# Rows of gathered experts placed by an estimate of VectorE's spare time, through the mixer and the dense experts

## The chip, the cores and the metric

The kernel runs on one core of a Trainium2 chip. A core has TensorE (PE, with its weight loads as PEld), VectorE (DVE), ScalarE (ACT), GpSimd (POOL) and SyncE (SP), each with an instruction queue of its own that is worked off in order, and 16 DMA engines that all of them share. The metric is the device time of one execution in microseconds (us), as the median of the runs.

## The reference

One layer of a decoder with 1024 tokens of 1024 channels, then a final norm:

```
h = rms_norm(x)
x = x + hybrid_mixer(h)          # stick-breaking attention, sparse attention, HGRN2, merge gates, w_out
h = rms_norm(x)
x = x + peer_ffn(h)
out = rms_norm(x)

# peer_ffn: 16384 experts, each a row of u_tab and a row of v_tab; 8 heads pick 16 experts each for every token
eidx, gate = ...                               # 128 experts a token, by the product of two key lists
hpre = einsum("nd,nhkd->nhk", xc, u_tab[eidx])
act  = gate * gelu(hpre)
y    = einsum("nhk,nhkd->nd", act, v_tab[eidx])
```

## The kernel before

**Parts.** The tokens are four parts of 256 (`PARTS`), that is eight tiles of 128. The parts go through the mixer one after the other, interleaved in 492 steps. In each step a few stages of the attention chains are emitted, and then further pieces (projections, norms, key scores, routes) up to a budget of VectorE and TensorE work.

**Two ways through the experts.** The middle parts (`DENSE`, tiles 2 to 5) go through all 16384 experts on TensorE. There are 128 first keys, and each takes one `gemm1` (24 matmuls of 512 columns, L242), splits of the weights into two float16 halves on ScalarE and VectorE (L200, L201), a product with the spread gates (L1368), and 24 matmuls of `gemm2` (L1375). Every fourth key adds a part kept in SBUF (L1383). At the end come four small final norms (L1395, L1398). The outer parts (tiles 0, 1, 6 and 7) gather their experts instead: for each of a tile's 128 choices one indirect DMA on GpSimd's queue brings 128 rows of 1024 floats (512 KB), one row for each token, and one VectorE instruction uses them. Such a transfer with its instruction is called a row here. A tile has 128 rows of `u` (L1104 and L1106) and then 128 of `v` (L1114 and L1116), so the four tiles have 1024 rows, all of which are emitted last in the program:

```
for c in range(128):
    vr = rows(f"v{ti}_{c}")                                   # one of RB = 5 buffers
    G.indirect_dma_start(out=vr, ..., in_=a["peer_v"], ...)   # L1114
    with paced():
        V.scalar_tensor_tensor(acc, in0=vr, scalar=act[:, c:c + 1], in1=acc, ...)   # L1116
```

The accumulator `acc` (called gacc in the profile) and, during the `u` rows, the tile's activations (gh) come from the same five buffers, so four are left for rows in flight. After a tile's last `v` row come its final norm and one store (L1119, L1120).

**What sets the order.** Each engine's order is fixed when the program is built: a scheduler with estimated times places the instructions, and emission order is their priority, so the rows come last in rank. `paced()` gives each row's VectorE instruction a lower bound: it may not stand ahead of a given VectorE instruction, the last one of some step. `mark()` is called at the end of each step and records that instruction with the step's estimated VectorE work `v` and TensorE work `p`. In the kernel before, `paced()` spreads 420 rows (`PACE`) over the mixer's steps from 135 on in proportion to `p + 3.0`, and leaves the other 604 with the mixer's last step as their only bound.

Tiles 0 and 1 know their experts after the first part's routes, which run beside the second part's mixer. Tiles 6 and 7 know theirs only when the last part's remaining pieces (merge, output projection, key scores, routes) have run, which is among the first keys of the dense experts.

Of the kernel before, what the change touches and what calls it, by code (L numbers as in the profile page):

```python
# [10 lines left out]
F32 = mybir.dt.float32  # L11
F16 = mybir.dt.float16
# [9 lines left out]
# the tensor and vector engines' work (us) that a step of the mixer is filled up to; the tensor engine's after the  # L22
# last step, and as a multiple of the vector engine's
RPE, RDVE, REND, PD = 3.5, 3.0, 5.0, 1.2
# the gathered rows that go beside the mixer: from which step on, how many, and a step's share besides its products
PACE0, PACE, PB = 135, 420, 3.0
# steps of the last part's tail for each block of dense experts; how far the first products run ahead
TP, LEAD = 3, 3
# buffers: gathered rows, weights, small tiles; banks for logits and transposes
# [7 lines left out]
# operands of the large products are split into two float16 parts after scaling by these powers of two  # L37
# [4 lines left out]
# scales of the gates, of their spread over the experts, and of the activations in the dense experts  # L42
# [5 lines left out]
# block numbers in the stream of projection weights  # L48
# [5 lines left out]
class Part:  # L54
    """a run of tokens that goes through the mixer together"""
# [8 lines left out]
# the parts whose tokens go through all experts; the others' experts are gathered  # L64
# [5 lines left out]
def trunk(ctx: ExitStack, tc: tile.TileContext, a: dict, out: bass.AP):  # L70
# [13 lines left out]
    # what the mixer alone needs  # L84
# [8 lines left out]
    def log_exp():  # L93
        """the activation table that holds both the logarithm and the exponential"""
        tc.keep_in_program_order(S.preload_act_table_set(LOG_EXP))
# [11 lines left out]
    def PT(shape, name):  # L107
        """a bank for transposes"""
        if mixing[0]:
            return ps_tr.tile(list(shape), F32, tag="tr", name=name)  # L110
        return ps_mm.tile(list(shape), F32, tag="mm", name=name)
# [17 lines left out]
    # strictly causal block in reversed key order: key 127 - x, allowed where 127 - x < p  # L129
# [3 lines left out]
    # causal block: key x allowed where p - x >= 0  # L133
# [3 lines left out]
    # for each length of segments: keys of a first half before queries of the second, the second halves' queries only  # L137
# [7 lines left out]
    # distances to the keys of the window and to the ends of the blocks, negative; far under where the key isn't seen  # L145
# [11 lines left out]
    # lower bounds: cumulative softmax over the layers less the first layer's share  # L157
# [12 lines left out]
    # the window's keys and values: this part's and the one's before  # L170
# [27 lines left out]
    def split(hi, lo, src, scale):  # L198
        """src * scale in two float16 parts"""
        S.activation(hi, src, AF.Copy, scale=scale)  # L200
        V.scalar_tensor_tensor(lo, in0=src, scalar=scale, in1=hi, op0=ALU.mult, op1=ALU.subtract)  # L201

    def rms_scale(src, name, junk, tg=""):
        """1/sqrt(mean(src^2) + eps) for each of 128 rows of 1024."""
# [15 lines left out]
    def load_w(blk, name, pt, br=False):  # L220
        """a block of weights in two parts; split for the first part, kept in DRAM for the others"""
# [29 lines left out]
    def transposed(src, name, pre=False):  # L251
        """the 128-column blocks of src transposed, side by side in one bank"""
# [11 lines left out]
    def norm_rows(xt, gname, nm):  # L264
        """RMSNorm of one token tile"""
        ht = W4(f"ht_{nm}")
        y = rms_scale(xt, nm, ht)
        V.scalar_tensor_tensor(ht, in0=xt, scalar=y, in1=gbc[gname], op0=ALU.mult, op1=ALU.mult)
        return ht

    def norm_cols(ht, hh, hl, tl, kk, scale, nm):
        """half of a token tile transposed into columns of hh / hl"""
# [24 lines left out]
    # Work comes in two kinds. Pieces stand on their own (projections, norms, merges); items are steps of the  # L297
    # branches' chains, each cut into four stages so that several can be under way at once.
# [37 lines left out]
    def sb_pieces(p, pt, st):  # L336
# [3 lines left out]
        def keep(t, d):  # L340
            # the tokens of earlier parts come back from DRAM
# [10 lines left out]
        # keys and values in reversed token order  # L352
# [19 lines left out]
    def sb_items(p, pt, st):  # L372
# [3 lines left out]
        def chunk(tl, hh, c0, c1, W):  # L376
# [17 lines left out]
            def weights():  # L394
                ee = x["ee"]
                # sum of softplus from the last key down, the key itself included
# [42 lines left out]
    def nsa_kv_pieces(pt, st):  # L439
# [22 lines left out]
        # compression of keys and values: block c takes the pieces c and c + 1 of 16 tokens.  # L462
        # Two neighbouring positions lie one under the other on the partitions; columns: position pair, group, block
# [3 lines left out]
        def pieces(which):  # L467
# [13 lines left out]
            # the last piece is kept for the next part  # L481
# [35 lines left out]
    def nsa_q_pieces(g, pt, st):  # L517
        gn = f"ns{pt.i}g{g}"

        def pq(i):  # L520
            # over the head's slope, a power of two: the distances then come in whole numbers, the same for all heads
# [8 lines left out]
    def nsa_items(g, tl, pt, st, kv):  # L530
# [9 lines left out]
        # compressed branch  # L540
        def c_logits():
# [6 lines left out]
            # a column of nothing before the first block  # L548
# [19 lines left out]
        def c_select():  # L568
            # importance of the blocks: the heads' weights of the five pieces that overlap; sure blocks at the top
# [7 lines left out]
            # the four best are struck out, by value and place  # L577
# [6 lines left out]
        def c_rows():  # L584
            # the block bias and the distance penalty as further rows of the queries
# [18 lines left out]
        # the selection is found and used while the window's heads go on  # L604
        res = [[c_logits, c_norm, c_turn, c_values], [None, c_select, None, None], None, [None, None, c_rows, None]]

        # window branch, then selected branch, one head at a time
        sums = {}

        def head(br, i):  # L610
# [9 lines left out]
            def logits():  # L620
# [3 lines left out]
                # logits, negative, and the least of them  # L624
# [77 lines left out]
    def hg_pieces(h, pt, st):  # L702
        """projections of a head: values token-major; gates raw"""
# [21 lines left out]
    def hg_items(h, pt, st):  # L725
# [10 lines left out]
        def decays():  # L736
            f = k = st["raw"][:, 0]
            V.tensor_scalar(f, f, olower[:, h:h + 1], lower[:, h:h + 1], op0=ALU.mult, op1=ALU.add)
            # log f; where f lies under the range of the logarithm's table, of f scaled up
# [25 lines left out]
        # attention within a chunk, by halves of ever shorter segments  # L765
        def level(lv):
# [7 lines left out]
            def spans():  # L774
                # both sides' distances to the middle
# [6 lines left out]
            def products():  # L782
                # keys on the first halves, queries (which lie n further) on the second
# [21 lines left out]
        # decays to the chunk's end and from its start  # L805
# [27 lines left out]
        # norm over the channels of the head, output gate  # L833
# [18 lines left out]
    def gate_pieces(r, pt, st):  # L852
        """six of the merge gates, raw"""
# [9 lines left out]
    def sigmoids(hg, mg, ng):  # L863
        """the sigmoids of a head of HGRN2, of six merge gates and of the sparse attention's gates, under one table"""
# [19 lines left out]
    def tail_pieces(pt):  # L884
# [17 lines left out]
        def wo(j):  # L902
            if j == 0:
                # at the end a buffer of the norm's is free
# [32 lines left out]
    def score_pieces(pt, st):  # L937
# [8 lines left out]
        def pq2(h):  # L946
# [3 lines left out]
            # the sixteen best of 128 and their places, in order  # L950
# [19 lines left out]
    def route(tile_no, ts_, ti_, gate):  # L970
        """best keys [128, 8, 2, 16] and their numbers -> first and second key of every expert [128, 128], gates [128, 8, 16]"""
# [9 lines left out]
        for h0 in (0, 4):  # L981
            # sums of the pairs (a, b) that can be among the sixteen best: all with (a + 1) * (b + 1) <= 16
# [18 lines left out]
        # gates  # L1001
# [7 lines left out]
        # place in the list -> (a, b)  # L1009
        V.tensor_copy(pf, p2)  # L1010
        # 0..31: a = pos >> 4, b = pos & 15
# [4 lines left out]
        # from 32: a = (pos >> 3) - 2, b = pos & 7; from 48: a = (pos >> 2) - 8, b = pos & 3; from 64: a = pos - 56, b = 0  # L1016
# [9 lines left out]
        # keys' numbers at (a, b): one-hot products, all whole numbers under 128  # L1026
# [27 lines left out]
    def account():  # L1054
        """estimates of what the vector and tensor engines have been given since the last call (us)"""
# [8 lines left out]
    total_ = [0.0, 0.0]  # L1064

    def mark():
        """a step's work: the vector engine's last instruction, and what the vector and tensor engines have to do"""
        account()
        v, p = load_["DVE"] - total_[0], load_["PE"] - total_[1]
        total_[:] = load_["DVE"], load_["PE"]  # L1070
        marks.append((next(i for i in reversed(nc.cur_bb.bb.instructions) if i.engine == mybir.EngineType.DVE), v, p))
# [3 lines left out]
    def paced():  # L1075
        """the next row's arithmetic waits for its turn among the mixer's"""
        if not paces:
            def rows(tau):
                return [tau * (p + PB) if k >= PACE0 else 0.0 for k, (_, v, p) in enumerate(marks)]

            lo, hi = 0.0, 10.0
            for _ in range(40):
                mid = (lo + hi) / 2
                lo, hi = (mid, hi) if sum(rows(mid)) < PACE else (lo, mid)
            acc = 0.0
            for m, r in zip(marks, rows(lo)):
                acc += r
# [408 lines left out]
```

## Time and profile before

| | |
|---|---|
| median of 3 runs | 3744.84 us |
| lowest and highest run | 3733.98 and 3757.71 us |
| profiled execution, first to last instruction | 3722.6 us |
| granted TensorE clock, mean | 0.921 |
| busy: TensorE, VectorE, ScalarE, GpSimd | 3285.9, 3035.8, 1572.2, 1275.4 us |
| moved by DMA | 1055.48 MB, 284 GB/s on average |

The profile is of one execution. Its span counts from the first to the last instruction; its own device time is not among the numbers at hand, and the three runs lie 11 to 35 us over the span. Engines overlap, so the busy times don't add up: what matters is which of them is full, or waited for, in each stretch. The mixer fills the time up to about 2100 us, then comes a stretch in which the last part's tail and the first dense keys mix, and from about 2490 us to 3676 us dense experts and gathered rows run side by side.

### The profile page before, as it was taken

The numbers are of one execution on the slowest core, as the hardware profiler recorded it, in microseconds if no ns is written. First come the engines' busy times: TensorE is split into PE (matmuls) and PEld (weight loads), VectorE is DVE, ScalarE is ACT, GpSimd is POOL, SyncE is SP. The second block draws the span as 40 slices with busy tenths as digits, with TensorE's granted clock in tenths as the row PEclk, the third lists the DMA queues.
The fourth block names the chain that finished last, engine by engine and source line by source line (L and its number), as shares of the span: only waits on it lengthen the run. The fifth ranks groups of instructions, "written<-read, shape, count | busy, mean of one in ns | idle before, by whom it ended". The sixth has DMA issues, their size and how long they took to land. (4 is left out here: it accounts for less than half of the span.)

```text
span 3722.6 us, 57637 instructions
## 1 busy us (share of the span) xinstructions
PE 3285.9 (88%) x20660; PEld 2191.0 (59%) x20660; DVE 3035.8 (82%) x7067; ACT 1572.2 (42%) x3110; POOL 1275.4 (34%) x1167
## 2 busy tenths in 40 slices
PE   6999999999986999898878897859999999999993
PEld 5887777777875777786566453424444444444441
DVE  5665689788799888789988678988888887888886
ACT  4776456554444564554457223323232223223222
POOL 0000002343322432233222344144555554555554
PEclk9999999999995999898577999979999999999996
DMA  7964857889974878877465999579999999999987
GB/s 260 334 243 144 295 189 274 317 308 325 328 273 147 300 256 300 296 278 261 142 208 195 356 332 325 193 273 339 333 337 325 320 337 322 346 332 318 334 287 261
DMA packets 359916, 1055.48 MB, mean 284 GB/s; under 512 B 35814, under 2 KB 108330, under 8 KB 355532
## 3 DMA queue, kind: packets, MB, share of 16 engines
q0 software_dynamic: 147456, 536.94, 41.5%
q1 hardware_dynamic: 212172, 514.86, 38.7%
q8 instruction: 162, 2.65, 0.3%
q14 instruction: 126, 1.03, 0.1%
HBM read 943.66 MB, written 108.00 MB: 283 GB/s over the span
## 5 line engine op out<-in xcount | busy, mean ns | idle before, releaser
L1114 POOL DMA_INDIRECT v<-in_peer_v_dram,gidx x512 | 655.1, 1280 | 872.7 <-DVE gacc L1116 590.8
L1104 POOL DMA_INDIRECT u<-in_peer_u_dram,gidx x512 | 605.9, 1183 | 869.1 <-DVE u L1106 599.4
L242 PE MATMUL g<-h,us 128*128 128x512 f16 x3072 | 712.5, 390 | 109.0 <-DVE acc L1383 71.4
L1116 DVE SCALAR_TENSOR_TENSOR gacc<-v,act,gacc 128x1024 f32<-128x1024 f32 x512 | 654.6, 1278 | 112.2 <-DMA v<-in_peer_v_dram,gidx 104.8
L1106 DVE SCALAR_TENSOR_TENSOR u<-u,gh 128x1024 f32<-128x1024 f32 x512 | 618.1, 1219 | 124.6 <-DMA u<-in_peer_u_dram,gidx 123.2
L242 PEld LDWEIGHTS <-us 128*128 128x128 f16 x3072 | 306.1, 100 | 497.8 <-issue 115.4
L1375 PE MATMUL acc<-vs,ac 128*128 128x512 f16 x2304 | 536.3, 384 | 33.1 <-ACT ac L200 28.4
L1375 PEld LDWEIGHTS <-ac 128*128 128x128 f16 x3072 | 302.9, 99 | 414.2 <-ACT ac L200 30.9
L242 PE MATMUL pj_mg<-hT,w_mg 128*128 128x256 f16 x2304 | 279.1, 277 | 16.3 <-ACT mg L859 9.5
L242 PEld LDWEIGHTS <-w_mg 128*128 128x128 f16 x2304 | 229.5, 101 | 48.8 <-issue 20.7
L200 ACT ACTIVATE vs<-vraw 128x1024 f16<-128x1024 f32 x128 | 133.8, 1048 | 270.3 <-DMA vraw<-in_peer_v_dram 270.1
L200 ACT ACTIVATE ac<-ge 128x512 f16<-128x512 f32 x128 | 79.9, 626 | 365.8 <-DVE ge L1368 250.0
L1335 ACT ACTIVATE ge<-g 128x512 f32<-128x512 f32 x128 | 75.6, 590 | 362.7 <-PE g L242 362.6
L1375 PE MATMUL g<-vs,ac 128*128 128x512 f16 x768 | 179.5, 385 | 9.6 <-DVE ts L958 7.3
L201 DVE SCALAR_TENSOR_TENSOR vs<-vraw,vs 128x1024 f16<-128x1024 f32 x128 | 155.2, 1217 | 23.2 <-ACT vs L200 23.2
L1174 PE MATMUL gb<-hot 128*128 128x128 f16 x512 | 126.3, 295 | 44.6 <-ACT stage L1177 28.9
L1177 ACT ACTIVATE stage<-gb 128x512 f32<-128x512 f32 x128 | 131.9, 1070 | 79.0 <-DMA d_G<-stage 45.2
L200 ACT ACTIVATE us<-uraw 128x1024 f16<-128x1024 f32 x128 | 134.0, 1049 | 68.2 <-DMA uraw<-in_peer_uT_dram 52.6
L242 PE MATMUL pb<-o,w_b 128*128 128x256 f16 x1152 | 141.6, 279 | 19.4 <-DMA w_b<-dw 9.3
L201 DVE SCALAR_TENSOR_TENSOR us<-uraw,us 128x1024 f16<-128x1024 f32 x128 | 155.7, 1218 | 2.9 <-ACT us L200 2.7
L242 PE MATMUL pj_r_hg<-hT,w_r_hg 128*128 128x256 f16 x1152 | 138.2, 277 | 1.5 <-ACT iv_hg L715 0.7
L242 PEld LDWEIGHTS <-w_b 128*128 128x128 f16 x1152 | 113.8, 101 | 42.6 <-issue 14.5
(1133 smaller groups left out, 5944.0 us busy)
## 6 DMA issues: line engine op xcount, KB each, us to landing
uraw<-in_peer_uT_dram SPq DMA_DIRECT2D x128, 512.0 KB, 6.7
vraw<-in_peer_v_dram SPq DMA_DIRECT2D x128, 512.0 KB, 6.2
w_mg<-dw SPq DMA_DIRECT2D x72, 512.0 KB, 6.3
d_G<-stage SPq DMA_DIRECT2D x32, 1024.0 KB, 5.1
gt<-d_G SPq DMA_DIRECT2D x32, 1024.0 KB, 13.2
w_r_hg<-dw SPq DMA_DIRECT2D x36, 512.0 KB, 5.7
w_b<-dw SPq DMA_DIRECT2D x72, 256.0 KB, 5.9
wr_mg<-in_wblk_dram SPq DMA_DIRECT2D x24, 512.0 KB, 5.1
```

The source lines that it names most:

```text
L200: S.activation(hi, src, AF.Copy, scale=scale)
L201: V.scalar_tensor_tensor(lo, in0=src, scalar=scale, in1=hi, op0=ALU.mult, op1=ALU.subtract)
L242: P.matmul(ps, l[:, k, :], r[:, k, :], start=(i == 0), stop=(i == n - 1))
L1104: G.indirect_dma_start(out=ur, out_offset=None, in_=a["peer_u"], in_offset=bass.IndirectOffsetOnAxis(ap=idx[:, c:c + 1], axis=0))
L1106: V.scalar_tensor_tensor(ur, in0=ur, scalar=1.0, in1=h2, op0=ALU.mult, op1=ALU.mult, accum_out=hpre[:, c:c + 1])
L1114: G.indirect_dma_start(out=vr, out_offset=None, in_=a["peer_v"], in_offset=bass.IndirectOffsetOnAxis(ap=idx[:, c:c + 1], axis=0))
L1116: V.scalar_tensor_tensor(acc, in0=vr, scalar=act[:, c:c + 1], in1=acc, op0=ALU.mult, op1=ALU.add)
L1174: P.matmul(ps[:, n, :], hs[:, 0, :, n], hs[:, 2, :, n], start=True, stop=False)
L1177: S.activation(stage[0][:, :, m0:m0 + 4].rearrange("p i n -> p n i"), ps, AF.Copy, scale=SA / SGT)
L1335: S.activation(ge, ps, AF.Gelu, scale=1.0 / (SW * SH2))
L1375: P.matmul(ps, ac[:, x, t * 128:(t + 1) * 128], v[:, y, dh * 512:(dh + 1) * 512], start=start and n == 0, stop=stop and n == 2)
```

## The change

`mark()` gets estimates of its own for each instruction, `paced()` a new rule, and marks are also set in the dense part: one ahead of it, and three for each first key (after `gemm1`, after the splits and the gate product, after `gemm2`). The new rule takes for each step the surplus of TensorE's estimated work over VectorE's, `max(p - v, 0)`, over the first 97% of all steps (`ROWS_BY`), multiplies it with one factor for all steps, and lets rows come in that proportion, never more than those whose experts are known by then (256 for each tile that has been routed). The factor is the smallest that brings all 1024 rows in. Rows beyond the list are bound to the step at 97%. No instruction is added, removed or changed; what can change is where the rows, and what the scheduler places around them, stand in each engine's order.

The core of the diff (comments that were taken out, and the constants `PACE0`, `PACE`, `PB` that fall away, are left out):

```diff
+ROWS_BY = 0.97
 def mark():
-    account()
-    v, p = load_["DVE"] - total_[0], load_["PE"] - total_[1]
-    total_[:] = load_["DVE"], load_["PE"]
-    marks.append((next(i for i in reversed(nc.cur_bb.bb.instructions) if i.engine == mybir.EngineType.DVE), v, p))
+    ins = nc.cur_bb.bb.instructions
+    v = p = 0.0
+    for i in ins[marked[0]:]:
+        if i.engine == mybir.EngineType.DVE:
+            aps = [x for x in [*i.outs, *i.ins] if len(getattr(x, "ap", ())) > 1]
+            n = max([math.prod([x[1] for x in o.ap[1:]]) for o in aps] or [0])
+            v += 0.09 + n / (1920.0 if aps and all(o.dtype in (F16, BF16) for o in aps) else 960.0)
+        elif i.engine == mybir.EngineType.PE:
+            n = math.prod([x[1] for x in i.outs[0].ap[1:]])
+            if i.ins[0].dtype != F32:
+                p += max(n / 2340.0, 0.11)
+            else:
+                p += 0.11 if getattr(i, "is_transpose", False) else 2 * max(n / 1170.0, 0.105)
+    marked[0] = len(ins)
+    marks.append((next(i for i in reversed(ins) if i.engine == mybir.EngineType.DVE), v, p))
 def paced():
     if not paces:
-        def rows(tau):
-            return [tau * (p + PB) if k >= PACE0 else 0.0 for k, (_, v, p) in enumerate(marks)]
-        lo, hi = 0.0, 10.0
+        spare = [max(p - v, 0.0) for _, v, p in marks[:int(len(marks) * ROWS_BY)]]
+        known = [256 * sum(r < k for r in known_.values()) for k in range(len(spare))]
+        def fill(f):
+            acc, res = 0.0, []
+            for w, n in zip(spare, known):
+                acc = min(acc + f * w, n)
+                res.append(acc)
+            return res
+        lo, hi = 0.0, 4.0
         for _ in range(40):
             mid = (lo + hi) / 2
-            lo, hi = (mid, hi) if sum(rows(mid)) < PACE else (lo, mid)
-        acc = 0.0
-        for m, r in zip(marks, rows(lo)):
-            acc += r
-            paces.extend([m[0]] * (int(acc) - len(paces)))
-        paces.append(marks[-1][0])
+            lo, hi = (mid, hi) if fill(mid)[-1] < 256 * len(known_) - 0.5 else (lo, mid)
+        for m, r in zip(marks, fill(hi)):
+            paces.extend([m[0]] * (int(r) - len(paces)))
+        paces.append(marks[len(spare)][0])
         paces.append(0)
...
     if pt not in DENSE:                       # routes(): a gathered tile's experts are known
         nc.sync.dma_start(d_gate[ti], gate)
+        known_[ti] = len(marks) + 2
...
+mark()                                        # ahead of the dense experts
 for k, i in enumerate(order):
     if k + LEAD < NI:
         ges[order[k + LEAD]] = gemm1(order[k + LEAD])
+        mark()
...
     split(ac[:, 0], ac[:, 1], ge, 1.0)
     group.append((ac, v))
+    mark()
...
     gone += 1
+    mark()                                    # after gemm2
```

More of the change, by code (lines that the diff above doesn't have):

```diff
@@ L24 @@
 RPE, RDVE, REND, PD = 3.5, 3.0, 5.0, 1.2
-PACE0, PACE, PB = 135, 420, 3.0
+ROWS_BY = 0.97
 TP, LEAD = 3, 3
@@ L1062, in account @@
         seen[0] = len(ins)
-    total_ = [0.0, 0.0]
+    marked = [0]
+    known_ = {}
     def mark():
-        account()
-        v, p = load_["DVE"] - total_[0], load_["PE"] - total_[1]
-        total_[:] = load_["DVE"], load_["PE"]
-        marks.append((next(i for i in reversed(nc.cur_bb.bb.instructions) if i.engine == mybir.EngineType.DVE), v, p))
+        ins = nc.cur_bb.bb.instructions
[13 more added lines that the diff above has]
+        marks.append((next(i for i in reversed(ins) if i.engine == mybir.EngineType.DVE), v, p))
     paces = []
```

## The prediction

> **What bounds the kernel now.** I read the page's busy times and groups first, then the windows, then the waits, last the end of the timeline.
>
> ```profile
> span 3722.6 us, 57637 instructions
> PE 3285.9 (88%) x20660; PEld 2191.0 (59%) x20660; DVE 3035.8 (82%) x7067; ACT 1572.2 (42%) x3110; POOL 1275.4 (34%) x1167
> PEclk9999999999995999898577999979999999999996
> L1116 DVE SCALAR_TENSOR_TENSOR gacc<-v,act,gacc 128x1024 f32<-128x1024 f32 x512 | 654.6, 1278 | 112.2 <-DMA v<-in_peer_v_dram,gidx 104.8
> L1106 DVE SCALAR_TENSOR_TENSOR u<-u,gh 128x1024 f32<-128x1024 f32 x512 | 618.1, 1219 | 124.6 <-DMA u<-in_peer_u_dram,gidx 123.2
> ```
>
> No engine is full over the whole span: TensorE is busy 88% of it, VectorE 82%. The 1024 rows are 1273 us of VectorE's 3036, so where they stand decides which engine is short in each stretch. By stretch (start, length, then busy us and count of each engine, granted clock, DMA share, GB/s):
>
> ```profile
> 1050.00:1200.00 150.00, 114.66 (x668) 90.21 (x668) 145.58 (x591) 55.76 (x145) 37.09 (x41) 0.71 0.60 199
> 1200.00:1675.00 475.00, 441.21 (x3437) 369.98 (x3436) 400.93 (x1002) 260.63 (x565) 152.47 (x147) 0.95 0.81 282
> 1675.00:1825.00 150.00, 121.78 (x708) 93.06 (x707) 145.83 (x593) 61.06 (x138) 40.24 (x38) 0.73 0.61 205
> 1825.00:2100.00 275.00, 231.96 (x1415) 171.54 (x1414) 224.23 (x500) 154.65 (x264) 75.01 (x60) 0.77 0.66 232
> 2100.00:2440.00 340.00, 288.63 (x1568) 158.28 (x1566) 284.93 (x669) 93.07 (x132) 118.62 (x105) 0.94 0.80 282
> 2440.00:2490.00 50.00, 25.02 (x96) 9.87 (x96) 43.65 (x147) 9.85 (x11) 24.70 (x20) 0.78 0.88 307
> 2490.00:3676.00 1186.00, 1103.46 (x4972) 492.48 (x4972) 987.93 (x1302) 327.59 (x423) 626.39 (x479) 0.96 0.92 325
> 3676.00:3723.00 47.00, 0.00 (x0) 0.00 (x0) 30.12 (x53) 20.50 (x30) 10.50 (x11) 0.54 0.69 237
> ```
>
> There are three regimes. In the two 150 us stretches, scores and routes fill VectorE (97%), while TensorE waits at about 0.72 of its clock. In the other mixer stretches neither is full (VectorE 84% and 82%, TensorE 93% and 84%). From 2490 us on TensorE is busy 93% and the DMA engines 92%; after 3676 us TensorE has nothing left. What limits the rows there is their buffers:
>
> ```profile
> POOL u L1104 <- DVE u L1106: 599.4, 297, 18.4
> POOL v L1114 <- DVE gacc L1116: 590.8, 289, 17.7
> DMA to landing us min/median/max: 4.1/6.4/11.4
> vraw<-in_peer_v_dram SPq DMA_DIRECT2D x100, 512.0 KB, 6.4
> ```
>
> GpSimd waits 1190 us for a VectorE row to free a buffer. With four buffers, a landing of 6.4 us (the third line, for L1114) and 1.28 us of VectorE, a row comes each (6.4 + 1.28) / 4 = 1.9 us at best. The last line, of the DMA view from 2490 to 3676 us, counts the keys there: one `vraw` a key, 100 keys in 1186 us, 11.9 us a key.
>
> **The change part by part.** Nothing is computed differently, so the question is only where rows go. I compared VectorE's order in the two built programs: the order gives each row its neighbours among the 4941 other VectorE instructions, and these have times in the trace of before. Rows by the stretch of before in which their neighbours ran:
>
> | stretch (us) | before | after | difference |
> |---|---|---|---|
> | up to 1050 | 159 | 158 | -1 |
> | 1050 to 1200 | 33 | 23 | -10 |
> | 1200 to 1675 | 126 | 108 | -18 |
> | 1675 to 1825 | 36 | 16 | -20 |
> | 1825 to 2100 | 58 | 32 | -26 |
> | 2100 to 2440 | 103 | 115 | +12 |
> | 2440 to 2490 | 20 | 7 | -13 |
> | 2490 to 3676 | 477 | 473 | -4 |
> | after 3676 | 12 | 92 | +80 |
>
> So 75 rows leave the mixer, the dense stretch takes none of them, and 80 more come after the last matmul; the last 72 follow each other with nothing between them.
>
> Why the dense part takes no more: in the new estimate a key has 24 matmuls of 512/2340 us, 5.25 us, in the mark of `gemm1` against a split of 1.16 us, then a mark with VectorE work alone, which counts as zero and not as negative, then 5.25 us of `gemm2` against some 0.3 us: 9 us of surplus, though TensorE's 10.5 less VectorE's 4.0 is 6.5. With the factor that the bisection arrives at, 0.65, the plan wants 5.9 rows a key up to key 118. Before runs 477 rows in 100 keys, 4.8 a key, with GpSimd waiting for buffers. The bound of `paced()` only holds rows back, it can't pull them ahead, so what falls behind the plan piles up at the end.
>
> *Gain, the two full stretches.* VectorE ends last there, and loses 10 `v` and 20 `u` rows:
>
> ```profile
> L1116 DVE SCALAR_TENSOR_TENSOR gacc<-v,act,gacc 128x1024 f32<-128x1024 f32 x33 | 41.9, 1269 | 0.0
> L1106 DVE SCALAR_TENSOR_TENSOR u<-u,gh 128x1024 f32<-128x1024 f32 x36 | 43.3, 1213 | 2.4 <-DMA u<-in_peer_u_dram,gidx 2.4
> PE trr L1145 <- DVE fb_rt L1041: 17.3, 1, 17.3
> ```
>
> 10 x 1.27 + 20 x 1.21 = 37 us. The third line (waits of TensorE from 1050 to 1200 us) shows what is released: TensorE sits 17.3 us for a route's last VectorE result. I count all 37.
>
> *Gain, the other two mixer stretches.* 18 + 26 rows at 1.25 us are 55 us of VectorE. TensorE's idle time there is 33.8 + 43.0 = 77 us, but VectorE idles too (74.1 and 50.8 us), so a row taken away sometimes shortens only a wait. Bounds 0 and 55; with both engines about equally near to full I take half, 27.
>
> *2100 to 2490 us.* 12 rows more and 13 fewer: zero, bounds -16 and +16 (13 rows at 1.25). *2490 to 3676 us.* 4 rows of 477: zero; buffers, DMA and TensorE are as before.
>
> *Loss, the end.* After 3676 us TensorE is done and covers nothing. Before ends like this (VectorE, GpSimd's store issue, and its landing):
>
> ```profile
> 3668.18 5.25 DVE L1116 SCALAR_TENSOR_TENSOR gacc<-v,act,gacc 128x1024 f32<-128x1024 f32 x4 [1.17 <-DMA v<-in_peer_v_dram,gidx]
> 3699.90 2.61 DVE L1116 SCALAR_TENSOR_TENSOR gacc<-v,act,gacc 128x1024 f32<-128x1024 f32 x2 [2.73 <-DMA v<-in_peer_v_dram,gidx]
> 3708.61 1.28 DVE L1119 SCALAR_TENSOR_TENSOR gacc<-gacc,gy_fin,gf 128x1024 f32<-128x1024 f32 x1
> 3709.93 0.34 SPq L1120 DMA_DIRECT2D out_dram<-gacc x1
> 3717.51 1.28 DVE L1398 SCALAR_TENSOR_TENSOR yd<-yd,y_find,gfd 128x1024 f32<-128x1024 f32 x1
> L1116 DVE SCALAR_TENSOR_TENSOR gacc<-v,act,gacc x29: 1275/1284/1286, 3640.3 to 3701.2; 128x1024 f32<-128x1024 f32 x29
> ```
>
> The price of a row with nothing beside it isn't in the trace. Below it is bounded by VectorE back to back, 5.25 / 4 = 1.31 us; landing 4.1 at the least gives (4.1 + 1.28) / 4 = 1.35. Above it is bounded by the 13 rows that the 47 us window holds: from 3676 to 3702.5 us, 2.04 us each, with small norms and their loads among them. With the dense transfers gone the landing should fall from 6.4, but four gathers in flight share the DMA engines, so I take the middle, 1.7: 80 x 1.7 = 136 us, bounds 105 and 163. From the last row to the end before needs 3722.6 - 3702.5 = 20.1 us, since two dense norms stand behind it. In the changed order these stand among the 80 rows, and only the tile's own norm follows: by 3710 its store is issued, some 3 us later it has landed, about 10 us in all. That saves 10.
>
> The Trainium skill, "DMA: Bandwidth & Descriptors", section on the anatomy of one DMA on GpSimd's path, gives 2.0 us plus the bytes at 436 GB/s for one transfer: an estimate of 3.2 us for 512 KB. The 512 landings here don't agree (none under 4.1). By that figure four buffers would never hold a row back, VectorE's 1.31 us would set the end, and the loss there would be 95 instead of 126.
>
> *Sum.* 136 - 10 - 37 - 27 = +62 us: a span of 3785, and 3744.8 + 62 = 3807 for the median of the runs, which lie 11 to 35 us over this span.
>
> **The rivals.**
>
> *Cheap end, full gain.* The rows at the end run at 1.31 us, since no other transfer competes, and each row taken from the mixer counts: 95 - 92 = +3, 3748 us. For it: most of the landing may be queueing. Against it: the 13 rows at 2.04 us, and VectorE's idle time in the mixer.
>
> *Faster: the mixer gives back more than the rows' own time.* VectorE takes its instructions in order, so a row that stands ahead of a chain's instruction also costs TensorE its wait and the time at lower clock after it. If all TensorE idle time of the four stretches went (35.3 + 33.8 + 28.2 + 43.0 = 140 us) and the end cost 95, it would be -45, 3700 us. It decides from the point at which the mixer gains more than the end costs, 95 to 126. Against it: 245.9 us of other VectorE work remain in the two full stretches next to 39 rows, and ScalarE and transfers end some of the other waits.
>
> *Nothing gained, dear end.* The mixer is held by TensorE at low clock and by its chains, the 75 rows only filled gaps, and the end runs at 2.04 us: 163 - 10 = +153, 3898 us. For it: VectorE's idle time outside the two full stretches; against it: the 17.3 us wait for the route.
>
> *It doesn't do what it says.* In the dense part this holds: 473 rows for 477 there. It is part of the forecast.
>
> **How the numbers follow.** The forecast has 0.70, the cheap end 0.15, faster 0.04, the dear end 0.11. The sum's bounds are 95 - 92 - 16 = -13 and 153 - 37 + 16 = +132. Eight in ten reach from +10 to +125: 3755 to 3870 us. About 1%, 37 us, is what a measurement of this kernel can tell from no change. Faster by more than that is 0.04; within it lies the cheap end and 0.02 of the forecast's lower end, 0.17; slower is 0.79.
>
> **What would show it.** The profile after should have TensorE at zero for 150 to 190 us at its end, with L1116 alone on VectorE there, 1.4 to 2.0 us apart; the first of the two full stretches shorter by about 12 us and the second by about 24; the last matmul 50 to 90 us earlier than 3676; and the dense keys at 11.9 us as now. I am wrong if the last matmul comes more than 95 us earlier, or if the rows at the end come faster than 1.4 or slower than 2.0 us.

## The result, and the profile after

The changed kernel takes 3856.16 us (median of 4 runs, 3828.85 to 3866.47) against 3744.03 us before. The ratio, here and below taken over all runs and not from the medians, is 1.0284 with a 95% interval of 1.0241 to 1.0327. It is slower by 112 us. Its profiled execution took 3854.28 us, 2 us over its span.

The page's head of the changed kernel (span, busy times, TensorE in 40 slices, costliest row group):

```profile
span 3852.3 us, 57672 instructions
PE 3278.6 (85%) x20660; PEld 2187.6 (57%) x20660; DVE 3049.3 (79%) x7067; ACT 1566.4 (41%) x3106; POOL 1280.8 (33%) x1167
PE   6999998999987899997887988899999998999700
L1135 DVE SCALAR_TENSOR_TENSOR gacc<-v,act,gacc 128x1024 f32<-128x1024 f32 x512 | 655.3, 1280 | 145.8 <-DMA v<-in_peer_v_dram,gidx 141.9
```

The work is the same to a per cent; the slices show two with no matmul at the end. The windows of the changed kernel (columns as before):

```profile
1050.00:1200.00 150.00, 119.43 (x733) 95.58 (x733) 145.13 (x621) 57.19 (x150) 29.32 (x34) 0.75 0.54 180
1200.00:1675.00 475.00, 442.57 (x3401) 366.82 (x3401) 376.06 (x919) 259.27 (x560) 128.48 (x128) 0.94 0.75 260
1675.00:1825.00 150.00, 125.02 (x787) 97.65 (x786) 136.14 (x599) 68.13 (x154) 20.98 (x20) 0.78 0.40 145
1825.00:2100.00 275.00, 230.38 (x1433) 170.02 (x1434) 197.77 (x478) 148.06 (x251) 39.75 (x35) 0.82 0.56 199
2470.00:3654.00 1184.00, 1101.15 (x4971) 492.10 (x4969) 977.29 (x1318) 332.69 (x430) 621.56 (x475) 0.97 0.92 324
3654.00:3853.00 199.00, 0.00 (x0) 0.00 (x0) 131.88 (x132) 20.61 (x30) 108.63 (x91) 0.51 0.79 266
```

In the mixer VectorE is less busy (198 us of 275 where it was 224, 376 of 475 where it was 401), and TensorE hardly more. The dense stretch is the old one. The last window, 47 us before, is 199 us now. The timeline of the end (TensorE's last two groups, then VectorE's first and last rows that stand alone, and the tile's norm):

```profile
3649.86 2.75 PE L1398 MATMUL g<-vs,ac 128*128 128x512 f16 x12
3652.45 1.46 PE L1398 MATMUL acc<-vs,ac 128*128 128x512 f16 x6
...
3703.19 1.28 DVE L1135 SCALAR_TENSOR_TENSOR gacc<-v,act,gacc 128x1024 f32<-128x1024 f32 x1
3704.87 1.28 DVE L1135 SCALAR_TENSOR_TENSOR gacc<-v,act,gacc 128x1024 f32<-128x1024 f32 x1 [0.41 <-DMA v<-in_peer_v_dram,gidx]
...
3839.59 2.60 DVE L1135 SCALAR_TENSOR_TENSOR gacc<-v,act,gacc 128x1024 f32<-128x1024 f32 x2 [1.25 <-DMA v<-in_peer_v_dram,gidx]
3847.21 1.28 DVE L1138 SCALAR_TENSOR_TENSOR gacc<-gacc,gy_fin,gf 128x1024 f32<-128x1024 f32 x1
```

So the account of the spans is: last matmul at 3653.9 instead of 3676.0 us, 22 earlier; from there to the end 198.4 instead of 46.6 us, 152 more; together +130. The runs move by 112. The old profile's span is 21 us under the median of its runs, and the changed kernel's runs lie only 2 us over their spans, so the old profile was of an execution some 19 us quicker than the median.

To see where a stretch gained I looked up the same VectorE instructions in the two traces. The table gives how much later they ran than in the trace of before (median over the instructions within 15 us of that time); the step from column to column is what a stretch cost. Below the changed kernel stand the experiments that follow. `old_mixer` and `before_five` have the old placing up to 1825 us and stay within 5 us there: so far the table can be trusted.

| kernel | 1050 us | 1200 | 1675 | 1825 | 2100 | 2490 | last matmul |
|---|---|---|---|---|---|---|---|
| changed | +9 | -2 | +6 | -9 | -11 | -27 | -22 |
| free_dense | -2 | -14 | -6 | -21 | -16 | +23 | +49 |
| old_mixer | -4 | -4 | -1 | -3 | +8 | -41 | -35 |
| drop72 | +7 | -3 | +1 | -14 | -19 | -34 | -23 |
| tail_buffers | +12 | +2 | +14 | -1 | -4 | -19 | -14 |
| small_rows | +3 | -21 | -42 | -56 | -50 | -65 | -65 |
| none_in_mixer | -21 | -49 | -76 | -103 | -120 | -79 | -68 |
| mixer_first | +5 | +62 | +109 | +112 | +108 | +61 | +68 |
| old_more | +7 | +57 | +67 | +83 | +74 | +31 | +31 |
| late_rows | +6 | +7 | +13 | +11 | +40 | +19 | +22 |
| fifth_buffer | -1 | 0 | +6 | +6 | +31 | +4 | -74 |
| before_five | -3 | -3 | -3 | -4 | 0 | -5 | -85 |
| changed_five | +4 | -6 | -1 | -17 | -19 | -31 | -103 |

### The profile page after: what moved, and what is told of

It reads as the page before. It is cut to its first block, busy times and chain, and to the rows that moved or that the text cites. A ratio compares the mean times of both kernels' runs of the same rounds, so it can differ in the third digit from the quotient of the medians.

```text
span 3852.3 us, 57672 instructions
## 1 busy us (share of the span) xinstructions
PE 3278.6 (85%) x20660; PEld 2187.6 (57%) x20660; DVE 3049.3 (79%) x7067; ACT 1566.4 (41%) x3106; POOL 1280.8 (33%) x1167
## 4 chain that ended last, share of the span: by engine, by line
PE 27%; issue 20%; DMA 18%; DVE 18%; POOL 11%; ACT 6%; SPq 0%; POOLq 0%; DVEq 0%; ACTq 0%
DMA v<-in_peer_v_dram,gidx 11%; POOL u L1123 8%; PE pj_mg L242 4%; DVE gacc L1135 3%; POOL v L1133 3%; PE pj_r_hg L242 3%; DMA u<-in_peer_u_dram,gidx 2%; PE pb L242 2%; DMA d_G<-stage 2%; DVE u L1125 2%; PE pj_wo L242 1%; PE z_sb L385 1%; PE gb L1194 1%; PE gb L1195 1%; ACT stage L1197 1%
## 5 line engine op out<-in xcount | busy, mean ns | idle before, releaser
L1123 POOL DMA_INDIRECT u<-in_peer_u_dram,gidx x512 | 619.4, 1210 | 1016.6 <-DVE u L1125 815.9
L1133 POOL DMA_INDIRECT v<-in_peer_v_dram,gidx x512 | 646.7, 1263 | 831.5 <-DVE gacc L1135 521.7
```

Source lines behind the costliest of these rows:

```text
L1123: G.indirect_dma_start(out=ur, out_offset=None, in_=a["peer_u"], in_offset=bass.IndirectOffsetOnAxis(ap=idx[:, c:c + 1], axis=0))
L1133: G.indirect_dma_start(out=vr, out_offset=None, in_=a["peer_v"], in_offset=bass.IndirectOffsetOnAxis(ap=idx[:, c:c + 1], axis=0))
```

## The experiments

Two theories were to be told apart. One: the end is what costs, 1.9 us for each row that stands alone, and the rows that left the mixer gain little. The other: the mixer's new placing itself costs, or gains much that something hides.

**The two halves of the change, one at a time.** `free_dense` keeps the new bounds in the mixer alone, `old_mixer` keeps the old ones in the mixer and the new ones behind it (`MIXED` is the number of mixer steps):

```diff
 # free_dense
-for m, r in zip(marks, fill(hi)):
+for m, r in zip(marks[:MIXED], fill(hi)):
     paces.extend([m[0]] * (int(r) - len(paces)))
-paces.append(marks[len(spare)][0])
+paces.append(marks[MIXED - 1][0])
 # old_mixer
+old = [p + 3.0 if k >= 135 else 0.0 for k, (_, v, p) in enumerate(marks[:MIXED])]
+acc = 0.0
+for m, w in zip(marks, old):
+    acc += 420.0 * w / sum(old)
+    paces.extend([m[0]] * (int(acc) - len(paces)))
 for m, r in zip(marks, fill(hi)):
```

> The changed kernel with the new bounds in the mixer alone; behind it the rows' only bound is the mixer's last step, as before the change. Counted from the order: the mixer's stretches have the changed kernel's rows up to 1825 us, the stretch from 2100 to 2490 us has 158 (122 in the changed kernel, 123 before), and 51 rows come after the last matmul instead of 92. Theory (the bounds in the dense part hold rows back, each row at the end costs 1.95 us, the full stretches' gain stays): 41 rows fewer at the end are 80 us off the changed kernel, less up to 20 for the fuller stretch from 2100 us on: 3776 to 3800 us. Rival (four buffers alone make the pile at the end, the bounds in the dense part do nothing): within 20 us of the changed kernel, 3836 to 3876.

Measured: 3836.35 us, 1.0244 of before (1.0213 to 1.0275). That is 36 us over the theory's range and at the rival's border, but the trace shows neither story whole. There are 52 rows after the last matmul and not 92, so the dense bounds do hold rows back. But the stretch from 2100 to 2490 us, with 35 rows more than before, got 39 us longer, a full VectorE price, and the dense stretch behind it took 26 us more with the same number of rows. Why the latter is so isn't settled; TensorE's wait for the accumulation of the second products there has grown from the 71.4 us of before, which is shown further down:

```profile
PE g L242 <- DVE acc L1407: 93.7, 24, 9.9
```

> The old bounds for the first 420 rows beside the mixer, the new ones behind it. By the order: 32, 127, 34 and 63 rows in the four mixer stretches from 1050 to 2100 us (33, 126, 36 and 58 before; 23, 108, 16 and 32 in the changed kernel), 47 from 2100 to 2490 us (123 before), 92 after the last matmul as in the changed kernel. Theory (the end is due to the dense part's bounds; the 75 rows that left the mixer gained about 22 us): the end costs the same 198 us after the last matmul, the mixer is as slow as before, so the time is that of the changed kernel plus 22, less up to 20 for the 76 rows missing from 2100 to 2490 us: 3855 to 3880 us. Rival (the mixer's new placing makes the loss): within 20 us of before, 3724 to 3764.

Measured: 3848.79 us, 1.0293 (1.0258 to 1.0327), 6 us under the theory's range. The mixer runs as before up to 1825 us (+1 from 1050 us; then +11 up to 2100 us, with 5 rows more), the last matmul comes 35 us earlier because 76 rows are missing from 2100 to 2490 us (step of -49), and the end takes 199 us. So the bounds in the dense part are enough for the whole loss, and the rival falls. But `free_dense`, which hasn't got them, loses 94 us against 107 here and 112 for both halves: the halves don't add up, each alone costs nearly what both do. In every order tried the dense stretch holds 471 to 479 rows, so rows that are kept out of the stretches ahead of it end up behind it.

**The end by itself.** `drop72` leaves out the 72 rows that stand alone:

```diff
-for c in range(128):
+for c in range(56 if ti == 7 else 128):     # the v rows
     vr = rows(f"v{ti}_{c}")
```

> The changed kernel without the last 72 v rows of the last tile, neither gathered nor added: the rows that stand alone at the end. What is left is the changed kernel up to its end with 20 rows after the last matmul, 12 before. Theory (72 x 1.93 us = 139 us stand alone): 139 less than the changed kernel, 3717 us or 27 under before, which is the gain that the mixer's part of the change makes. Rival (the mixer's part gains the 64 us of the prediction, and something else in the profiled execution hid it): 3680 us.

Measured: 3715.42 us, 0.9930 (0.9903 to 0.9958): 141 us less than the changed kernel, as the theory had it. What is left is 26 us under the 3741.82 us of before in the same runs, though it also does 72 rows less.

`tail_buffers` gives these rows six buffers in flight instead of four:

```diff
-vr = rows(f"v{ti}_{c}")
+vr = late.tile([128, D], F32, tag="vraw", bufs=2) if ti == 7 and c >= 58 and c % 3 == 0 else rows(f"v{ti}_{c}")
```

> The changed kernel with six buffers in flight instead of four for the rows at the end: every third v row of the last tile from number 58 on goes into one of the two buffers that held the dense experts' raw v weights. The order of the other work is the same. Theory (buffers set the pace: landing 5.6 us, VectorE 1.28 and the hand-over 0.27 in a round of four, 1.8 to 1.95 us a row; with six the DMA engines, 82% busy there, become the bound at 0.82 x 1.93 = 1.58 us): 72 x 0.35 = 25 us less than the changed kernel. Rival one (the DMA engines already set the pace, more in flight only lands later): no difference within 10 us. Rival two (VectorE sets the pace once buffers are there): 1.31 us a row, 45 us less.

Measured: 3829.03 us, 1.0233 (1.0195 to 1.0272), 27 us less than the changed kernel. From the first to the last of the rows alone a row takes 1.94 us in the changed kernel and 1.54 here. The windows of the rows alone, and the landing of their gathers, first in the changed kernel, then with six buffers:

```profile
3705.00:3842.00 137.00, 0.00 (x0) 0.00 (x0) 90.93 (x71) 0.00 (x0) 83.41 (x68) 0.50 0.82 275
DMA to landing us min/median/max: 4.6/5.6/6.8
```

```profile
3710.00:3820.00 110.00, 0.00 (x0) 0.00 (x0) 92.02 (x72) 0.00 (x0) 77.89 (x69) 0.50 0.95 346
DMA to landing us min/median/max: 5.0/6.1/6.7
```

With four buffers nothing is full: VectorE 66%, GpSimd 61%, DMA 82%. The round of a buffer sets the pace. With six the DMA engines are at 95%, and each gather lands later while more of them are under way. The Trainium skill, "DMA: Bandwidth & Descriptors", section on bandwidth, puts the HBM side at some 358 GB/s for a core. The 346 GB/s at 95% lie under it, but it isn't a ceiling here: in the dense stretch of before a slice of 30 us reached 382. The Trainium skill, "DMA: Bandwidth & Descriptors", section on the anatomy of one DMA on GpSimd's path, has a fixed 2.0 us plus the bytes at 436 GB/s, which makes an estimate of 3.2 us for such a gather. The trace doesn't agree: none landed under 4.6 us here.

**What a row costs in the mixer.** `small_rows` keeps the old order and every gather, and cuts the arithmetic of tile 0's `v` rows and tile 1's `u` rows from 1024 to 8 columns:

```diff
+w = 8 if ti == 1 else D                      # u rows; for the v rows: ti == 0
-V.scalar_tensor_tensor(ur, in0=ur, scalar=1.0, in1=h2, ...)
+V.scalar_tensor_tensor(ur[:, :w], in0=ur[:, :w], scalar=1.0, in1=h2[:, :w], ...)
```

> The kernel before, with 256 of its rows' arithmetic cut from 1024 to 8 columns: the v rows of tile 0 and the u rows of tile 1, which stand from about 950 to 1970 us. Their gathers stay, and the rows stand where they stood (33, 126, 36 and 65 in the four mixer stretches against 33, 126, 36 and 58). Theory one (a row costs its VectorE time in the two full stretches, and little where ScalarE, TensorE or transfers end the waits): the two full stretches get 33 x 1.2 = 40 and 36 x 1.15 = 41 us shorter, the other two together by 0.3 us for each of 184 rows, 55 us; 3742 - 136 = 3606 us. Theory two (VectorE's order is what everything waits for, a row costs its 1.2 us anywhere): 3742 - 256 x 1.17 = 3442 us. Rival (VectorE is not the bound in the mixer at all): 3742 within 20.

Measured: 3667.09 us (0.9792, 0.9744 to 0.9841), 77 us less: not the 136 of the expectation's theory one, and far from its theory two. By the table, the first full stretch loses 24 us with 33 cheap rows, the second 14 with 36, the one between 21 with 126, and the last none. The four stretches of `small_rows`, at their own times:

```profile
1050.00:1180.00 130.00, 105.27 (x743) 85.64 (x742) 116.83 (x605) 56.26 (x147) 34.89 (x42) 0.86 0.68 245
1180.00:1630.00 450.00, 422.71 (x3345) 355.38 (x3344) 275.06 (x990) 254.47 (x554) 129.79 (x147) 0.96 0.82 294
1630.00:1770.00 140.00, 120.95 (x813) 96.23 (x813) 114.69 (x606) 62.73 (x145) 37.09 (x38) 0.83 0.67 232
1770.00:2045.00 275.00, 225.28 (x1364) 166.36 (x1364) 197.67 (x502) 154.22 (x263) 80.20 (x64) 0.75 0.68 238
```

From 1180 to 1630 us VectorE is down from 84% to 61% of the time, and 126 cheap rows have bought 21 us. Even in the "full" stretches VectorE falls to 90% and 82%: it was full because of the rows, with another limit close behind.

`none_in_mixer` binds every row to the mixer's last step:

```diff
+paces.append(marks[MIXED - 1][0])            # the only bound that is left
-for m, r in zip(marks, fill(hi)): ...
-paces.append(marks[len(spare)][0])
```

> All rows' bounds are at the mixer's last step or later: none up to 1825 us, 17 up to 2100 us, 166 from 2100 to 2490 us, 475 in the dense stretch, 366 after the last matmul (12 before). Theory (row prices: about 22 us gained for the 75 rows that the change took from the mixer, 0.3 us each, and 1.95 us for a row at the end): the mixer ends 412 x 0.3 = 120 us earlier or a little more, the stretch from 2100 us on is 43 rows fuller (+45 us), the end costs 354 x 1.95 = 690 us: 3742 - 120 + 45 + 690 = 4357 us. Rival (a row in the mixer costs its whole 1.25 us of VectorE): the mixer ends 515 us earlier, 3962 us.

Measured: 4341.07 us (a single run). The mixer ends 120 us earlier for 395 rows, 0.3 us a row, and the rows at the end stand alone for 723 us:

```profile
3608.00:4331.00 723.00, 0.00 (x0) 0.00 (x0) 479.95 (x537) 23.48 (x33) 436.76 (x368) 0.50 0.83 276
```

With 367 rows that is 1.97 us each. Both prices of the theory hold over a range some five times that of the change.

**More rows in the mixer.** `mixer_first` raises the new rule's factor to at least 0.95 in the mixer, `old_more` raises the old rule's 420 rows to 470 and skips steps with more VectorE than TensorE work; both leave the dense part free:

```diff
 # mixer_first
-acc = min(acc + f * w, n)
+acc = min(acc + (max(f, 0.95) if k < MIXED else f) * w, n)
 # old_more
+shares = [(p + 3.0 if p > v else 0.0) if k >= 144 else 0.0 for k, (_, v, p) in enumerate(marks[:MIXED])]
```

> The changed kernel's surplus rule with a factor of at least 0.95 in the mixer, and the rows that don't fit there bound to the mixer's last step alone. By the order: 80, 143, 0 and 107 rows in the four mixer stretches (33, 126, 36, 58 before), 22 and 19 in the two up to 2490 us (103 and 20 before), 478 in the dense stretch, 14 after the last matmul (12 before). Theory (prices by stretch from the runs so far: about 1.1 us in the first full stretch, 0.75 in the second, little from 1200 to 1675 and 1825 to 2100 us, 0.5 to 1 from 2100 to 2440 us, 1.95 at the end): +52 - 27 + 10 - 60 + 4 = -21, 3721 us, 3700 to 3742. Rival (what sets the time is only how many rows stand at the end): within 10 us of before.

> The rule before the change (by the step's TensorE work plus 3.0) with 470 rows beside the mixer instead of 420, from step 144 on, and no share for steps whose estimated VectorE work is over TensorE's; no bounds in the dense part. By the order: 70, 143, 10 and 99 rows in the four mixer stretches (33, 126, 36, 58 before), 30 and 19 up to 2490 us (103 and 20), 478 in the dense stretch, 14 at the end. Theory (the same prices by stretch): +41 - 20 + 10 - 55 + 4 = -20, 3722 us, 3700 to 3742. Rival (only the rows at the end count): within 10 us of before.

Measured: 3796.89 us (1.0139, 1.0093 to 1.0184) and 3761.03 us (1.0047, 1.0028 to 1.0067), 55 and 19 us over the theory's range. Part of the expected counts was wrong. Counted as the rows that ran between the table's columns, the four mixer stretches hold 79, 168, 36 and 50 rows in `mixer_first` and 70, 142, 49 and 61 in `old_more`, so the second full stretch (36 before) was emptied in neither. And my prices failed: with 46 and 37 rows more in the first full stretch it got 57 and 50 us longer, 1.2 and 1.35 us a row, where the rows taken away had gained 1.1. From 1200 to 1675 us, 42 and 16 rows more cost 47 and 10 us, and 13 more in `old_more`'s second full stretch cost 16, where I had put next to nothing and a gain. The first full stretch of `old_more`:

```profile
1050.00:1250.00 200.00, 119.67 (x708) 93.44 (x707) 191.38 (x646) 53.84 (x140) 90.46 (x79) 0.67 0.77 253
```

VectorE is 96% busy there over 200 us instead of 150. A row taken out of the mixer gains 0.3 us on average, a row put in can cost its whole 1.25 us or more: the old placing stands near the point where VectorE becomes the bound. Skipping steps by `p > v` doesn't keep rows out of a full stretch, since a bound holds back but can't expel what has fallen behind.

**Late rows, and a fifth buffer.** `late_rows` is the kernel before with 1.6 times the share in the mixer's last 76 steps; `fifth_buffer` is that, with a fifth buffer in flight for the rows of tiles 6 and 7, taken from the split `v` weights:

```diff
 # late_rows
-return [tau * (p + PB) if k >= PACE0 else 0.0 ...]
+return [tau * (p + PB) * (1.6 if k >= 416 else 1.0) if k >= PACE0 else 0.0 ...]      # PACE 460
 # fifth_buffer
-vr = rows(f"v{ti}_{c}")                      # and the u rows likewise
+vr = late.tile([128, D], F32, tag="rowx", bufs=1) if ti > 5 and c % 5 == 4 else rows(f"v{ti}_{c}")
-v = late.tile([128, 2, D], F16, tag="v", bufs=6)
+v = late.tile([128, 2, D], F16, tag="v", bufs=5)
```

> The kernel before with 1.6 times the share of rows in the mixer's last 76 steps and the old placing ahead of them. By the order: 158, 33, 126 and 35 rows up to 1825 us as before, 77 instead of 58 from 1825 to 2100 us, 83 instead of 103 from 2100 to 2440 us, 13 instead of 12 at the end. Theory (a row that comes into a stretch with room costs 0.3 us, one that leaves the stretch from 2100 us on saves 0.65): +6 - 13 + 2 = -5, 3739 us, 3729 to 3747. Rival (whatever is added to the mixer costs VectorE's whole 1.25 us, as in the two kernels that put more rows there): +24 - 13 + 2 = +13, 3757 us.

> The same with a fifth buffer in flight for the rows of the last two tiles, taken from the split v weights, which get five buffers instead of six; the order stays the same but for a few rows (479 in the dense stretch, 10 at the end). Theory (in the dense stretch TensorE and the DMA engines, at 93% and 92%, set the pace, and the buffers only the rows, which keep up with it): within 10 us of the kernel without the fifth buffer. Rival (VectorE's waits for landings, 169 us in the stretch from 2100 us on, hold the matmuls up, and the fifth buffer takes a fifth of them away): 20 to 30 us less.

Measured: `late_rows` 3749.58 us (1.0014, 0.9993 to 1.0034), no change that can be told. By the table two prices cancel in it: the 19 rows more from 1825 to 2100 us cost 29 us, 1.5 us a row and not the theory's 0.3, and the 20 fewer from 2100 to 2490 us gave 21 back, more than either side had put. `fifth_buffer` 3651.54 us (0.9771, 0.9736 to 0.9807): 98 us less than `late_rows`, and my theory was wrong, the rival right and even too small. The last pair takes the fifth buffer alone, without and with the change:

> The kernel before with the fifth buffer for the last two tiles' rows and nothing else. By the order the mixer is as before, 26 rows stand from 2440 to 2490 us (20), 479 in the dense stretch (477), 4 after the last matmul (12). Theory (four buffers make rows land late, VectorE waits for them in order, and TensorE for VectorE; a fifth gives 70 us in the dense stretch, and the end has 8 rows fewer): 3742 - 74 - 16 = 3652 us, 3635 to 3665. Rival (the gain needs the later rows of the other kernel): over 3690.

> The changed kernel with the fifth buffer for the last two tiles' rows. By the order 472 rows in the dense stretch and 93 after the last matmul, as without it. Theory (the same dense gain; at the end five in flight make 1.6 us a row instead of 1.94): 3856 - 70 - 30 = 3756 us, 3735 to 3775, still 90 to 115 over the kernel before with the same buffer. Rival (the dense bounds leave VectorE its waits whatever the buffers): 3856 - 30 = 3826 us, 3805 to 3840.

Measured: 3630.56 us (0.9702, 0.9677 to 0.9727), 4 us under the theory's range, and 3755.03 us (1.0019, 1.0000 to 1.0038), within it. The waits of TensorE in the dense stretch, from 2490 us on, before:

```profile
PE g L242 <- DVE acc L1383: 71.4, 20, 10.6
```

and with the fifth buffer alone, with the window of the whole stretch, which runs there from 2485 to 3592 us:

```profile
PE g L242 <- DVE us L201: 19.7, 1, 19.7
PE g L242 <- DVE acc L1383: 14.9, 7, 5.6
2485.00:3592.00 1107.00, 1081.51 (x4972) 488.05 (x4972) 989.80 (x1303) 329.91 (x425) 673.35 (x481) 0.99 0.96 351
```

The same 4972 matmuls take 1107 us instead of 1186; a key has 48 of them, so it takes 10.7 us instead of 11.4. A row that hasn't landed stops VectorE, which works in order; the accumulation of the second products stands behind it, and TensorE waits for that one. With the buffer VectorE's waits for landings in the stretch fall from 138 to 56 us, and this wait of TensorE from 71 to 15; that the one makes the other is inferred from the order. TensorE is now busy 98%. `before_five` is the kernel that beats both, by 3.0% and by 226 us against the changed one. In the presence of the fifth buffer the change costs 124 us, 1.69 us for a row alone, and the rest of the account is unchanged: the buffer doesn't repair the placing.

## Why the prediction was right, and where it was off

**The direction and the cause: right.** The end has 92 rows after the last matmul, `drop72` puts the price of 72 of them at 141 us, and the dense stretch is what it was. That the dense part's bounds hold rows back is shown by `free_dense`, and that they are enough for the loss by `old_mixer`; that the mixer's bounds without them cost nearly as much wasn't foreseen. That the surplus was over-estimated at 9 us a key is read from the code; no run tried another estimate. And the rows a key come from the scheduler's fixed order, not from the chip's buffers as I argued: with five buffers the order still has 472 rows there, and the chip runs them faster.

Of the signs named, the first full stretch (11 us shorter), the pace of the keys and that of the rows at the end (1.94 us) came out. The second full stretch gained 15 us and not 24, the last matmul came 22 us earlier and not 50 to 90, and TensorE stands idle for 198 us and not 150 to 190. +112 us lies near the top of +10 to +125: the range was wide enough, the sum of +62 was not well sized, and the end and the mixer erred in the same direction.

**The end: under-sized.** I took 1.7 us for a row alone; it is 1.94, and the end costs 152 us more than before, against 126. The landing is not what failed: 1.7 stands for a landing of 5.5 us, and 5.6 came. The step that failed is the round of a buffer taken as landing and VectorE alone, (5.6 + 1.28) / 4 = 1.72. Some 0.9 us of a round of 4 x 1.94 are left, and they are the hand-over: in the trace the next gather into a buffer starts 0.7 us after the row before has ended, on average, and a row begins 0.15 us after its landing. That is 17 us over the 72 rows alone. Most of the rest lies with the first 20 of the 92 rows, which stand among the dense norms and took 2.4 us each.

Three figures in the prediction were read wrongly. The window from 3676 us has 12 rows after the one that began at 3675.05, at 2.18 us each, not 13 at 2.04, so the bound above should have been 174. The other VectorE work of the two full stretches is 291 - 85 = 206 us, not 245.9. And the dense window has 100 loads, but its 4972 matmuls are 103.6 keys of 48, so a key took 11.4 us and 4.6 rows, not 11.9 and 4.8. None of them changes the forecast's side.

**The gain in the mixer: over-sized.** Forecast were 64 us, measured 20 (five kernels with the new placing gave 20, 14, 26, 16 and 23 from 1050 to 2100 us). By stretch, with the same five: the first full one 10 to 12 for 13 forecast, the second 15 to 16 for 24, the others between a gain of 1 and a loss of 13 where 27 were to be gained. The step that failed is "VectorE ends last there" taken at the full price of each row: `small_rows` shows that VectorE stops being the bound after the first rows are gone, and that outside these two stretches its time is worth 0.2 us a row or nothing.

Why the others lost stays open. One place where it can be seen is around 1325 us, first before, then after:

```profile
1325.00:1350.00 25.00, 22.60 (x183) 19.10 (x182) 16.64 (x32) 21.02 (x43) 5.05 (x5) 0.91 0.72 263
1350.00:1375.00 25.00, 23.94 (x189) 19.12 (x189) 23.55 (x53) 12.20 (x28) 8.29 (x6) 0.89 0.70 234
```

```profile
1325.00:1350.00 25.00, 18.72 (x127) 15.01 (x127) 10.38 (x22) 22.28 (x44) 2.25 (x3) 0.80 0.47 167
1350.00:1375.00 25.00, 23.49 (x200) 18.85 (x198) 23.50 (x49) 10.66 (x23) 10.03 (x7) 0.93 0.63 211
```

From 1325 to 1350 us ScalarE is busy 84% and 89%, and VectorE has room. The change left 1 of 5 rows there, and TensorE did fewer matmuls in that time and not more. VectorE is 94% busy in the 25 us behind, before and after, so what cost the time isn't told by these windows. An estimate from TensorE's and VectorE's work alone doesn't see ScalarE.

**2100 to 2490 us: at the bound.** Zero was forecast, 16 us came, all of it after 2440 us, where 13 rows left 50 us with VectorE at 87%; the 12 rows more up to 2440 us cost next to nothing.

**The rivals.** The dear end, with 0.11, was as near as the forecast or nearer: its 3898 us are 42 too many where the forecast's 3807 are 49 too few, and its end of +153 came out at 152. Its zero for the mixer was wrong by 20 us from 1050 to 2100 us, the forecast's 64 by 44. The cheap end and the faster case asked for a mixer gain of 92 and 140 us; taking all rows out of the mixer gave 120.

## What to carry to other kernels

A lower bound in an order can only delay: what falls behind a plan collects at the end, where it has no cover, so a plan's rate has to be one that the order really reaches. Price a piece of work by the stretch it leaves and by the one it enters: out of the mixer a row was worth 0.3 us, into it up to 1.5, alone at the end 1.94, though its VectorE time is 1.25 everywhere. Where an engine that works in order waits for landings, look first at how many transfers are in flight: one more buffer was worth 3.0%, more than any placing tried here.

## What the runs showed of the hardware

A gather of 128 rows of 4 KB lands after 5.6 us (4.6 at the least) even when only three others are under way and next to nothing else moves; with six in flight it takes 6.1 us, and the core moves 346 GB/s instead of 275. And VectorE's waits for landings, 138 us in the dense stretch of the kernel before,

```profile
DVE u L1106 <- DMA u<-in_peer_u_dram,gidx: 73.6, 65, 2.9
DVE gacc L1116 <- DMA v<-in_peer_v_dram,gidx: 64.3, 58, 3.7
```

came with waits of TensorE, which uses nothing of what lands there: one more buffer shortened both and took 79 us off that stretch.
